# Expert blocks in a new order, and expert weights in half-size pieces

## Chip, cores and metric

The kernel runs on one core of a Trainium2 chip. The metric is the device time of one execution in microseconds (us). Engines are called as in the profile: PE multiplies (PEld loads its weights), DVE and ACT are the two engines for elementwise work on SBUF and PSUM, POOL is a slower third one that also issues indirect transfers, SP issues the plain transfers. Sixteen DMA engines move the data.

## The reference, cut to what matters

The reference is two transformer blocks on 1024 tokens of width 1024. Everything up to the last step (projections, convolution, a recurrent branch, attention, the router) is untouched here. The last step is a mixture of 32 experts. Each token goes to its two best experts; tokens are grouped by expert into blocks of 128 rows, and a block is computed as

```
def expert_block(args):
    xb, e = args
    hb = jax.nn.silu(xb @ w_gate[e]) * (xb @ w_up[e])     # 128x1024 @ 1024x256, twice
    return hb @ w_down[e]                                  # 128x256 @ 256x1024
```

after which each token's two results are weighted and added to the residual.

## The kernel before, in words

The expert step is phase_m. It always runs 33 blocks: one for each expert e = 0 to 31 (the first 128 tokens routed to it), and one, number 32 = NE, for the first expert that got more than 128. A loop under a run-time condition does further blocks; with these inputs it isn't entered.

A block needs 3 MB of float32 weights, 1 MB for each of gate, up and down, of which every partition gets 8 KB in one run. Products are made at near float32 accuracy from float32r halves: every operand x is split into h, a rounded copy (ACT, L1502 and L99), and l = x - h (DVE, L1503 and L100), and the product is h·h + h·l + l·h. The steps of a block, with the names of the profile:

- gather: POOL fetches the block's 128 token rows by index into mx (L1591, three buffers).
- moe_in: PE transposes mx in eight pieces (L1517); ACT and DVE split the result into xh and xl.
- weight_split: for gate, up and down in turn, SP issues the load of 1 MB into a buffer mw (L1608, three buffers in all), ACT makes gh or dh, DVE makes the rest ml (five buffers). For block 0 POOL does the subtraction in DVE's place; for block 32 the loads are indirect transfers issued by POOL (L1599).
- moe_up: 8 steps of four products each into one PSUM bank (L1529, L1531 twice, L1532); then ACT's silu (L1534) and DVE's product (L1535) give hb.
- moe_down: two transposes of hb (L1544), a split into hh and hl, twelve products into two PSUM banks (L128 to L130), each evicted to my by ACT (L1553); POOL scatters the rows to Y (L1595).

The program order is: prepare block e+1 (moe_in, the gather for e+2, all three weights), moe_up of e+1, moe_down of e. The framework that builds the program takes this order as a priority and reorders each engine's instructions by when it reckons them ready, so an engine's queue isn't exactly the program order; but once built, each engine and each issuing queue works strictly in its own order, and an instruction that waits holds up those behind it. A load can be issued only when the mw buffer that it takes has been read by both ACT and DVE. PSUM gives three banks named pm, which moe_up and moe_down share.

Before phase_m stands the router, a long chain of small DVE operations that ends in the token lists; the loads and splits of block 0 run beside it. route_rest, which places the tokens beyond the first 128 of an expert, is issued with block 6. After the last block, combine loads Y (8 MB), adds and stores the result (L1565 to L1570).

Of the kernel before, what the change touches and what calls it, by code (L numbers as in the profile page):

```python
# [1401 lines left out]
def route_rest(g, r, rt):  # L1402
# [41 lines left out]
    v.tensor_copy(rt["wi"], oex)  # L1444
# [46 lines left out]
def weight_split(g, wp, raw, wraw, eng=None):  # L1491

    nc = g.nc
    gh = wp.tile([128, 8, 512], F32R, name="gh", tag="gh", bufs=2)
    dh = wp.tile([128, 2, D], F32R, name="dh", tag="dh", bufs=2)
    ls = []
    for i, (w, h) in enumerate((("gate", gh[..., :256]), ("up", gh[..., 256:]), ("down", dh))):
        rw = raw.tile([128, 2048], F32, name="mw", tag="mw", bufs=3)
        wraw(w, rw)
        split = lambda x: x.rearrange("p (a b) -> p a b", a=8 if i < 2 else 2)  # L1500
        l = split(raw.tile([128, 2048], F32R, name="ml", tag="ml", bufs=5))
        nc.scalar.activation(h, split(rw), AF.Copy)  # L1502
        (eng or nc.vector).tensor_tensor(l, split(rw), b32(h), op=OP.subtract)  # L1503
        ls.append(l)
    return gh, ls[:2], dh, ls[2]
# [17 lines left out]
def moe_up(g, mp, xs, ws):  # L1523
    nc = g.nc
    xh, xl = xs
    gh, gl = ws[:2]
    p = pm(g)
    for j in range(8):
        nc.tensor.matmul(p, xh[:, j], gh[:, j], start=j == 0, stop=False)  # L1529
        for i in range(2):  # L1530
            nc.tensor.matmul(p[:, i * 256:i * 256 + 256], xh[:, j], gl[i][:, j], start=False, stop=False)  # L1531
        nc.tensor.matmul(p, xl[:, j], gh[:, j], start=False, stop=j == 7)  # L1532
    hb = mp.tile([128, 256], F32, name="hb", tag="hb", bufs=3)
# [5 lines left out]
def moe_down(g, mp, hb, ws, ydst):  # L1539
    nc = g.nc  # L1540
    dh, dl = ws[2:]
    pt = pg(g, 2, 128)
    for j in range(2):
        nc.tensor.transpose(pt[:, j], hb.rearrange("p (f j) -> p j f", j=2)[:, j, :], g.ident)  # L1544
    hh = mp.tile([128, 2, 128], F32R, name="hh", tag="hh", bufs=2)
    hl = mp.tile([128, 2, 128], F32R, name="hl", tag="hl", bufs=2)
    split_psum(g, hh, hl, pt)
    y = mp.tile([128, D], F32, name="my", tag="my", bufs=2)
    for n in range(2):
        p = pm(g)  # L1550
        for j in range(2):
            mm3(nc, p, hh[:, j], hl[:, j], dh[:, j, HALF[n]], dl[:, j, HALF[n]], j == 0, j == 1)
        nc.scalar.activation(y[:, HALF[n]], p, AF.Copy)  # L1553
# [3 lines left out]
def combine(g, raw, rt, res, k0, dst):  # L1557
# [4 lines left out]
    for t in range(NT):  # L1562
        tag, bufs = ("mw", 3) if t < 3 else ("ml", 5)
        ys.append(raw.tile([128, 2, D], F32, name="fy", tag=tag, bufs=bufs))
        nc.sync.dma_start(ys[t], src[tcol(t)])  # L1565
    for t in range(NT):
        h = res(t)
        for k in range(2):
            nc.vector.scalar_tensor_tensor(h, ys[t][:, k], rt["c"][:, k0 + k, t:t + 1], h, op0=OP.mult, op1=OP.add)  # L1569
# [12 lines left out]
def phase_m(g, acc, r, rt, out, mp, wp, raw):  # L1582
# [4 lines left out]
          "down": ins["w_down"].rearrange("e (p j) f -> (e p) (j f)", j=2)}  # L1587

# [9 lines left out]
    def gathered(idx):  # L1598
        return lambda w, rw: nc.gpsimd.indirect_dma_start(out=rw, out_offset=None, in_=wv[w], in_offset=off(idx))  # L1599
# [3 lines left out]
    mx = [mp.tile([128, D], F32, name=f"mx{i}") for i in range(3)]  # L1603
# [3 lines left out]
    def prep(e):  # L1607
        src = gathered(rt["wi"][:, 0:1]) if e == NE else lambda w, rw: nc.sync.dma_start(rw, wv[w][tcol(e), :])  # L1608
        xs = moe_in(g, mx[e % 3], xt.pop() if xt else moe_xt(mp))
        if e < NE:  # L1610
            gather(mx[(e + 1) % 3], rt["tok"][:, e + 1:e + 2])
        return weight_split(g, wp, raw, src, nc.gpsimd if e < 1 else None), xs

    gather(mx[0], rt["tok"][:, 0:1])
    ws, xs = prep(0)
    hb = moe_up(g, mp, xs, ws)
    for e in range(NE + 1):
        if e == 6:
            route_rest(g, r, rt)
        cur = hb, ws  # L1620
        if e < NE:
            ws, xs = prep(e + 1)
# [240 lines left out]
```

## Time and profile before

| | us |
|---|---|
| median of 3 runs (2861.75 to 2862.96) | 2862.53 |
| the profiled execution, its own time | 2861.98 |
| its span, first to last instruction | 2860.3 |
| hb of block 0 made | 2446.6 |
| hb of block 32 made | 2816.1 |

The span is what the trace shows, the time is what is measured around it; they differ by 1.7 us. The distance of the two hb marks holds 32 blocks in steady work, 11.55 us each; before it lie the earlier phases and the start of the expert step, behind it the last moe_down and combine.

### The profile page before, as it was taken

Reading aid. Unit: us, or ns where it says so; the run is one execution under the profiler, and the core shown is the slowest. Engines: PE = TensorE matmul, PEld = TensorE weight load, DVE = VectorE, ACT = ScalarE, POOL = GpSimd, SP = SyncE. Lnnn points to the kernel's source line nnn. Section 1 sums busy time; section 2 is a strip of 40 time slices with the busy share of each in tenths; the row PEclk is TensorE's granted clock in tenths of the full one; section 3 lists DMA queues with packets and bytes.
Section 4 is the critical chain, followed back from the end, with each engine's and each line's share of the span. In section 5 each row is a group of like instructions: output and inputs, shape, how many; then the busy total and the mean of one; then the engine's idle time right before and its main releaser. Section 6 shows DMA issues by size and latency. Waiting matters only on the chain. (4 is left out here: it accounts for less than half of the span.)

```text
span 2860.3 us, 33815 instructions
## 1 busy us (share of the span) xinstructions
PE 2672.9 (93%) x13274; PEld 2213.2 (77%) x13274; DVE 1850.0 (65%) x2551; ACT 1151.8 (40%) x1703; POOL 272.1 (10%) x290
## 2 busy tenths in 40 slices
PE   8999999999899999999999999998899996889894
PEld 6888888888778888777888878997777774777773
DVE  5778988898873332366254241677777777777775
ACT  4112121112122221455244332556767653667672
POOL 3000000000000000020000000000111113312111
PEclk9999999999999999999999999999999998999997
DMA  3111111111135432431122241444122214788987
GB/s 136 44 37 38 54 50 39 43 52 45 37 110 188 174 118 67 155 118 63 65 65 70 81 166 47 154 136 164 62 86 78 71 36 170 262 284 301 318 318 273
DMA packets 107905, 341.34 MB, mean 119 GB/s; under 512 B 15072, under 2 KB 35808, under 8 KB 95072
## 3 DMA queue, kind: packets, MB, share of 16 engines
q1 hardware_dynamic: 97808, 319.22, 32.3%
q0 software_dynamic: 9936, 19.94, 2.0%
q8 instruction: 105, 1.72, 0.3%
q14 instruction: 56, 0.46, 0.1%
HBM read 272.52 MB, written 84.41 MB: 125 GB/s over the span
## 5 line engine op out<-in xcount | busy, mean ns | idle before, releaser
L122 ACT ACTIVATE wh<-wr 128x1024 fp32r<-128x1024 f32 (+2 forms) x161 | 164.5, 1023 | 560.8 <-PE pm L129 423.2
L123 DVE TENSOR_TENSOR wl<-wr,wh 128x1024 fp32r<-128x1024 f32 (+2 forms) x159 | 187.6, 1182 | 289.1 <-ACT wh L122 288.5
L128 PE MATMUL pm<-uh,wh 128*128 128x512 f32 x896 | 360.3, 402 | 5.1 <-DVE gz L449 4.2
L129 PE MATMUL pm<-ul,wh 128*128 128x512 f32 x896 | 356.7, 398 | 0.3 <-DVE ul L103 0.3
L130 PE MATMUL pm<-uh,wl 128*128 128x512 f32 x896 | 355.4, 397 | 0.0
L277 DVE SCALAR_TENSOR_TENSOR acc<-v,vec,acc 128x1024 f32<-128x1024 f32 x240 | 307.4, 1281 | 3.9
L128 PE MATMUL pm<-nth,wh 128*128 128x512 f32 (+1 forms) x656 | 261.2, 398 | 0.7 <-ACT nth L102 0.7
L130 PE MATMUL pm<-nth,wl 128*128 128x512 f32 (+1 forms) x656 | 260.5, 397 | 0.0
L129 PE MATMUL pm<-ntl,wh 128*128 128x512 f32 (+1 forms) x656 | 258.5, 394 | 0.0
L128 PEld LDWEIGHTS pm<-uh,wh 128*128 128x128 f32 x896 | 170.5, 190 | 41.0 <-DVE gz L449 4.6
L130 PEld LDWEIGHTS pm<-uh,wl 128*128 128x128 f32 x896 | 170.5, 190 | 35.4 <-issue 1.0
L129 PEld LDWEIGHTS pm<-ul,wh 128*128 128x128 f32 x896 | 170.6, 190 | 35.0 <-issue 1.4
L1503 DVE TENSOR_TENSOR ml<-mw,gh 128x2048 fp32r<-128x2048 f32 x64 | 146.4, 2290 | 44.3 <-ACT gh L1502 44.2
L1502 ACT ACTIVATE gh<-mw 128x2048 fp32r<-128x2048 f32 x66 | 126.4, 1917 | 65.0 <-DMA mw<-in_w_up 34.6
L129 PEld LDWEIGHTS pm<-ntl,wh 128*128 128x128 f32 (+1 forms) x656 | 122.1, 186 | 31.2
L130 PEld LDWEIGHTS pm<-nth,wl 128*128 128x128 f32 (+1 forms) x656 | 122.0, 186 | 30.9
L128 PEld LDWEIGHTS pm<-nth,wh 128*128 128x128 f32 (+1 forms) x656 | 122.1, 186 | 30.2 <-ACT nth L102 0.9
L100 DVE TENSOR_TENSOR ptl<-pa,pth 128x512 fp32r<-128x512 f32 (+4 forms) x160 | 100.4, 633 | 60.2 <-ACT pth L99 59.6
L1531 PEld LDWEIGHTS pm<-ml,xh 128*128 128x128 f32 x528 | 105.3, 200 | 38.3 <-DVE ml L1503 15.0
L1529 PE MATMUL pm<-gh,xh 128*128 128x512 f32 x264 | 111.6, 423 | 19.5 <-ACT my L1553 18.5
L1531 PE MATMUL pm<-ml,xh 128*128 128x256 f32 x528 | 117.8, 297 | 10.8 <-DVE ml L1503 10.8
L1532 PE MATMUL pm<-gh,xl 128*128 128x512 f32 x264 | 109.0, 413 | 0.0
(520 smaller groups left out, 5958.2 us busy)
## 6 DMA issues: line engine op xcount, KB each, us to landing
wr<-in_w_in SPq DMA_DIRECT2D x97, 512.0 KB
mw<-in_w_gate SPq DMA_DIRECT2D x32, 1024.0 KB
mw<-in_w_up SPq DMA_DIRECT2D x32, 1024.0 KB
mw<-in_w_down SPq DMA_DIRECT2D x32, 1024.0 KB
Y<-zero SPq DMA_DIRECT2D x4, 2048.0 KB
fy<-Y SPq DMA_DIRECT2D x8, 1024.0 KB
kd<-kv SPq DMA_DIRECT2D x32, 192.0 KB
qd<-qs SPq DMA_DIRECT2D x32, 192.0 KB
```

The lines of the kernel that those rows point to most:

```text
L100: nc.vector.tensor_tensor(l, src, b32(h), op=OP.subtract)
L122: nc.scalar.activation(h, raw, AF.Copy)
L123: (eng or nc.vector).tensor_tensor(l, raw, b32(h), op=OP.subtract)
L128: nc.tensor.matmul(out, lh, rh, start=first, stop=False)
L129: nc.tensor.matmul(out, lh, rl, start=False, stop=False)
L130: nc.tensor.matmul(out, ll, rh, start=False, stop=last)
L277: nc.vector.scalar_tensor_tensor(acc, v[:, j:j + T], w[:, j:j + 1], acc, op0=OP.mult, op1=OP.add)
L1502: nc.scalar.activation(h, split(rw), AF.Copy)
L1503: (eng or nc.vector).tensor_tensor(l, split(rw), b32(h), op=OP.subtract)
L1529: nc.tensor.matmul(p, xh[:, j], gh[:, j], start=j == 0, stop=False)
L1531: nc.tensor.matmul(p[:, i * 256:i * 256 + 256], xh[:, j], gl[i][:, j], start=False, stop=False)
L1532: nc.tensor.matmul(p, xl[:, j], gh[:, j], start=False, stop=j == 7)
```

## The change

The loop now looks two blocks ahead. In iteration e it brings and splits gate and up of block e+2, does the first half of moe_up of e+1, then the transposes and the split of hb of block e (moe_hidden, in the middle of moe_up), the second half of moe_up, then moe_in of e+2, then brings and splits down of e+1, then the products of moe_down of e. Each weight comes in two transfers of 512 KB, 4 KB a partition, into mw buffers of half the size (eight instead of three large ones), with eight ml buffers and one more of half the size instead of five large ones. The splits are done by halves too, so there are twice as many instructions on ACT and DVE for them, each on 1024 instead of 2048 elements a partition. mx has two buffers, not three. For block 32 the row index of the indirect loads is kept for either half (rt["wi"]). combine loads Y in 16 pieces of 512 KB instead of 8 of 1 MB.

```diff
--- before.py
+++ after.py
@@ -1441,7 +1441,10 @@
     v.tensor_reduce(oex, ib, axis=AX.X, op=OP.add)
     v.tensor_scalar(oex, oex, 31.0, None, op0=OP.min)
     v.scalar_tensor_tensor(oex, oex, 128.0, r["part"].to_broadcast([128, 16]), op0=OP.mult, op1=OP.add)
-    v.tensor_copy(rt["wi"], oex)
+
+    for half in range(2):
+        v.tensor_scalar(ib[:, 0, :16], oex, 2.0, float(half), op0=OP.mult, op1=OP.add)
+        v.tensor_copy(rt["wi"][:, half], ib[:, 0, :16])
     ibk = til("ibk", 8, 16)
     nc.gpsimd.iota(ibk, pattern=[[0, 8], [1, 16]], base=0, channel_multiplier=0, allow_small_or_imprecise_dtypes=True)
     pt = pm(g)
@@ -1488,21 +1491,29 @@
     slot_tokens(g, r, pt, rt, 32, 16)
 
 
-def weight_split(g, wp, raw, wraw, eng=None):
-
-    nc = g.nc
+def gate_up(g, wp, raw, wraw, eng=None):
+
     gh = wp.tile([128, 8, 512], F32R, name="gh", tag="gh", bufs=2)
+    return gh, [halved(g, raw, wraw, w, gh[..., i * 256:i * 256 + 256], 4, eng) for i, w in enumerate(("gate", "up"))]
+
+
+def down(g, wp, raw, wraw, eng=None):
     dh = wp.tile([128, 2, D], F32R, name="dh", tag="dh", bufs=2)
+    return dh, halved(g, raw, wraw, "down", dh, 1, eng)
+
+
+def halved(g, raw, wraw, w, h, n, eng):
     ls = []
-    for i, (w, h) in enumerate((("gate", gh[..., :256]), ("up", gh[..., 256:]), ("down", dh))):
-        rw = raw.tile([128, 2048], F32, name="mw", tag="mw", bufs=3)
-        wraw(w, rw)
-        split = lambda x: x.rearrange("p (a b) -> p a b", a=8 if i < 2 else 2)
-        l = split(raw.tile([128, 2048], F32R, name="ml", tag="ml", bufs=5))
-        nc.scalar.activation(h, split(rw), AF.Copy)
-        (eng or nc.vector).tensor_tensor(l, split(rw), b32(h), op=OP.subtract)
+    for half in range(2):
+        rw = raw.tile([128, 1024], F32, name="mw", tag="mw", bufs=8)
+        wraw(w, half, rw)
+        split = lambda x: x.rearrange("p (a b) -> p a b", a=n)
+        l = split(raw.tile([128, 1024], F32R, name="ml", tag="ml", bufs=9))
+        hh = h[:, half * n:half * n + n]
+        g.nc.scalar.activation(hh, split(rw), AF.Copy)
+        (eng or g.nc.vector).tensor_tensor(l, split(rw), b32(hh), op=OP.subtract)
         ls.append(l)
-    return gh, ls[:2], dh, ls[2]
+    return ls
 
 
 def moe_xt(mp):
@@ -1520,36 +1531,43 @@
     return xh, xl
 
 
-def moe_up(g, mp, xs, ws):
+def moe_up(g, mp, xs, ws, mid=None):
     nc = g.nc
     xh, xl = xs
-    gh, gl = ws[:2]
+    gh, gl = ws
     p = pm(g)
     for j in range(8):
         nc.tensor.matmul(p, xh[:, j], gh[:, j], start=j == 0, stop=False)
         for i in range(2):
-            nc.tensor.matmul(p[:, i * 256:i * 256 + 256], xh[:, j], gl[i][:, j], start=False, stop=False)
+            nc.tensor.matmul(p[:, i * 256:i * 256 + 256], xh[:, j], gl[i][j // 4][:, j % 4], start=False, stop=False)
         nc.tensor.matmul(p, xl[:, j], gh[:, j], start=False, stop=j == 7)
+        if j == 3 and mid:
+            mid()
     hb = mp.tile([128, 256], F32, name="hb", tag="hb", bufs=3)
     nc.scalar.activation(hb, p[:, :256], AF.Silu)
     nc.vector.tensor_tensor(hb, p[:, 256:], hb, op=OP.mult)
     return hb
 
 
-def moe_down(g, mp, hb, ws, ydst):
-    nc = g.nc
-    dh, dl = ws[2:]
+def moe_hidden(g, mp, hb):
+
     pt = pg(g, 2, 128)
     for j in range(2):
-        nc.tensor.transpose(pt[:, j], hb.rearrange("p (f j) -> p j f", j=2)[:, j, :], g.ident)
-    hh = mp.tile([128, 2, 128], F32R, name="hh", tag="hh", bufs=2)
-    hl = mp.tile([128, 2, 128], F32R, name="hl", tag="hl", bufs=2)
-    split_psum(g, hh, hl, pt)
+        g.nc.tensor.transpose(pt[:, j], hb.rearrange("p (f j) -> p j f", j=2)[:, j, :], g.ident)
+    hs = [mp.tile([128, 2, 128], F32R, name="h" + x, tag="h" + x, bufs=2) for x in "hl"]
+    split_psum(g, *hs, pt)
+    return hs
+
+
+def moe_down(g, mp, hs, ws, ydst):
+    nc = g.nc
+    hh, hl = hs
+    dh, dl = ws
     y = mp.tile([128, D], F32, name="my", tag="my", bufs=2)
     for n in range(2):
         p = pm(g)
         for j in range(2):
-            mm3(nc, p, hh[:, j], hl[:, j], dh[:, j, HALF[n]], dl[:, j, HALF[n]], j == 0, j == 1)
+            mm3(nc, p, hh[:, j], hl[:, j], dh[:, j, HALF[n]], dl[j][:, 0, HALF[n]], j == 0, j == 1)
         nc.scalar.activation(y[:, HALF[n]], p, AF.Copy)
     ydst(y)
 
@@ -1560,13 +1578,14 @@
     src = g.Y.rearrange("(k t) d -> t k d", k=2)
     ys = []
     for t in range(NT):
-        tag, bufs = ("mw", 3) if t < 3 else ("ml", 5)
-        ys.append(raw.tile([128, 2, D], F32, name="fy", tag=tag, bufs=bufs))
-        nc.sync.dma_start(ys[t], src[tcol(t)])
+        tag, bufs = ("mw", 8) if t < 4 else ("ml", 9)
+        ys.append([raw.tile([128, D], F32, name="fy", tag=tag, bufs=bufs) for _ in range(2)])
+        for k in range(2):
+            nc.sync.dma_start(ys[t][k], src[tcol(t), k])
     for t in range(NT):
         h = res(t)
         for k in range(2):
-            nc.vector.scalar_tensor_tensor(h, ys[t][:, k], rt["c"][:, k0 + k, t:t + 1], h, op0=OP.mult, op1=OP.add)
+            nc.vector.scalar_tensor_tensor(h, ys[t][k], rt["c"][:, k0 + k, t:t + 1], h, op0=OP.mult, op1=OP.add)
         nc.sync.dma_start(dst[tcol(t), :], h)
 
 
@@ -1585,6 +1604,9 @@
     wv = {"gate": ins["w_gate"].rearrange("e (p j) f -> (e p) (j f)", j=8),
           "up": ins["w_up"].rearrange("e (p j) f -> (e p) (j f)", j=8),
           "down": ins["w_down"].rearrange("e (p j) f -> (e p) (j f)", j=2)}
+    wh = {"gate": ins["w_gate"].rearrange("e (p h j) f -> (e p h) (j f)", h=2, j=4),
+          "up": ins["w_up"].rearrange("e (p h j) f -> (e p h) (j f)", h=2, j=4),
+          "down": ins["w_down"].rearrange("e (p h) f -> (e p h) f", h=2)}
 
     def gather(x, idx):
 
@@ -1596,47 +1618,70 @@
                                      oob_is_err=False)
 
     def gathered(idx):
-        return lambda w, rw: nc.gpsimd.indirect_dma_start(out=rw, out_offset=None, in_=wv[w], in_offset=off(idx))
+        return lambda w, half, rw: nc.gpsimd.indirect_dma_start(out=rw, out_offset=None, in_=wh[w], in_offset=off(idx(half)))
 
 
     xt = [moe_xt(mp)]
-    mx = [mp.tile([128, D], F32, name=f"mx{i}") for i in range(3)]
+    mx = [mp.tile([128, D], F32, name=f"mx{i}") for i in range(2)]
     for x in mx:
         nc.gpsimd.memset(x, 0.0)
 
-    def prep(e):
-        src = gathered(rt["wi"][:, 0:1]) if e == NE else lambda w, rw: nc.sync.dma_start(rw, wv[w][tcol(e), :])
-        xs = moe_in(g, mx[e % 3], xt.pop() if xt else moe_xt(mp))
-        if e < NE:
-            gather(mx[(e + 1) % 3], rt["tok"][:, e + 1:e + 2])
-        return weight_split(g, wp, raw, src, nc.gpsimd if e < 1 else None), xs
-
-    gather(mx[0], rt["tok"][:, 0:1])
-    ws, xs = prep(0)
-    hb = moe_up(g, mp, xs, ws)
+    def src(e):
+        if e == NE:
+            return gathered(lambda half: rt["wi"][:, half, 0:1])
+        return lambda w, half, rw: nc.sync.dma_start(rw, wv[w][tcol(e), half * 1024:half * 1024 + 1024])
+
+    def bring(e):
+        if e <= NE:
+            gather(mx[e % 2], rt["tok"][:, e:e + 1])
+
+
+    def ready(e):
+        x = moe_in(g, mx[e % 2], xt.pop() if xt else moe_xt(mp))
+        bring(e + 2)
+        return x
+
+    eng = lambda e: nc.gpsimd if e < 1 else None
+    for e in range(2):
+        bring(e)
+    gu = {0: gate_up(g, wp, raw, src(0), eng(0))}
+    dn = {0: down(g, wp, raw, src(0), eng(0))}
+    xs = {0: ready(0)}
+    gu[1] = gate_up(g, wp, raw, src(1))
+    hb = moe_up(g, mp, xs.pop(0), gu.pop(0))
+    xs[1] = ready(1)
     for e in range(NE + 1):
         if e == 6:
             route_rest(g, r, rt)
-        cur = hb, ws
+        hs = []
+        if e + 2 <= NE:
+            gu[e + 2] = gate_up(g, wp, raw, src(e + 2))
         if e < NE:
-            ws, xs = prep(e + 1)
-            hb = moe_up(g, mp, xs, ws)
-        moe_down(g, mp, *cur, lambda y: scatter(y, rt["row"][:, e:e + 1]))
+            hb = moe_up(g, mp, xs.pop(e + 1), gu.pop(e + 1), lambda hb=hb: hs.append(moe_hidden(g, mp, hb)))
+        else:
+            hs.append(moe_hidden(g, mp, hb))
+        if e + 2 <= NE:
+            xs[e + 2] = ready(e + 2)
+        if e < NE:
+            dn[e + 1] = down(g, wp, raw, src(e + 1))
+        moe_down(g, mp, hs[0], dn.pop(e), lambda y: scatter(y, rt["row"][:, e:e + 1]))
     combine(g, raw, rt, lambda t: acc[:, t], 0, out)
 
 
     n = nc.values_load(rt["more"][0:1, 0:1], min_val=0, max_val=15)
     with tc.If(n > 0):
-        cur, tmp = (r["pool"].tile([128, 3, 16], I32, name=n, tag=tag) for n, tag in (("cur", "ib"), ("curt", "sel")))
-        for i, x in enumerate((rt["tok"][:, 32:48], rt["wi"], rt["row"][:, 32:48])):
+        cur, tmp = (r["pool"].tile([128, 4, 16], I32, name=n, tag=tag) for n, tag in (("cur", "ib"), ("curt", "sel")))
+        for i, x in enumerate((rt["tok"][:, 32:48], rt["wi"][:, 0], rt["row"][:, 32:48], rt["wi"][:, 1])):
             nc.vector.tensor_copy(cur[:, i], x)
         with tc.For_i(0, n, 1):
             nc.vector.tensor_copy(tmp, cur)
             nc.vector.tensor_copy(cur[:, :, 0:15], tmp[:, :, 1:16])
-            ws = weight_split(g, wp, raw, gathered(cur[:, 1, 0:1]))
+            from_ = gathered(lambda half: cur[:, 2 * half + 1, 0:1])
+            gu = gate_up(g, wp, raw, from_)
+            dn = down(g, wp, raw, from_)
             gather(mx[0], cur[:, 0, 0:1])
-            hb = moe_up(g, mp, moe_in(g, mx[0], moe_xt(mp)), ws)
-            moe_down(g, mp, hb, ws, lambda y: scatter(y, cur[:, 2, 0:1]))
+            hb = moe_up(g, mp, moe_in(g, mx[0], moe_xt(mp)), gu)
+            moe_down(g, mp, moe_hidden(g, mp, hb), dn, lambda y: scatter(y, cur[:, 2, 0:1]))
         combine(g, raw, rt, lambda t: acc[:, t], 2, out)
 
 
@@ -1696,7 +1741,7 @@
                 nc.vector.tensor_scalar(t[:96], t[:96], -96 ** -0.5, None, op0=OP.mult)
             small[nm + "g"] = t
         rt = {"c": c.tile([128, 4, 8], F32, name="rtc"), "row": c.tile([128, NB], I32, name="rtr"),
-              "tok": c.tile([128, NB], I32, name="rtt"), "wi": c.tile([128, 16], I32, name="rtw"),
+              "tok": c.tile([128, NB], I32, name="rtt"), "wi": c.tile([128, 2, 16], I32, name="rtw"),
               "more": c.tile([1, 1], I32, name="rtm")}
         chs = ExitStack()
         with ExitStack() as s:
```

## Rows read from the trace of the kernel before

**Rows 1.** The page, 40 equal slices of the span: busy tenths of PE and of DMA.

```profile
PE   8999999999899999999999999998899996889894
DMA  3111111111135432431122241444122214788987
```

**Rows 2.** DVE's product hb: duration min/median/max in ns, first and last start in us.

```profile
L1535 DVE TENSOR_TENSOR hb<-pm,hb x33: 414/418/425, 2446.6 to 2816.1; 128x256 f32<-128x256 f32 x33
```

**Rows 3.** Busy time of stretches; last columns: granted PE clock, DMA share, GB/s.

```profile
2446.60:2816.10 369.50, 329.75 (x1720) 274.59 (x1719) 274.02 (x230) 253.50 (x250) 76.69 (x62) 0.95 0.85 300
...
2738.00:2753.00 15.00, 13.21 (x69) 10.79 (x69) 11.39 (x9) 11.58 (x13) 3.05 (x3) 1.00 0.97 373
...
2826.00:2856.00 30.00, 0.00 (x0) 0.00 (x0) 20.23 (x16) 0.00 (x0) 0.00 (x0) 0.50 1.02 408
...
4.00:12.00 8.00, 2.07 (x6) 0.87 (x6) 2.90 (x4) 5.66 (x9) 4.15 (x8) 1.00 1.02 411
```

**Rows 4.** Waits, 2446.6 to 2816.1: engine, line, releaser, total us, times, longest.

```profile
DVE ml L1503 <- ACT gh L1502: 44.2, 39, 4.1
...
ACT gh L1502 <- DMA mw<-in_w_up: 31.6, 17, 4.4
ACT gh L1502 <- DMA mw<-in_w_gate: 23.2, 20, 2.2
PEld pm L1529 <- ACT my L1553: 23.1, 11, 3.9
```

**Rows 5.** Timeline, SP, ACT and DVE: one mw buffer's round.

```profile
2642.82 0.33 SPq L1608 DMA_DIRECT2D mw<-in_w_gate  x1
...
2651.13 1.92 ACT L1502 ACTIVATE gh<-mw 128x2048 fp32r<-128x2048 f32 x1 [1.59 <-DMA mw<-in_w_gate]
...
2653.09 2.29 DVE L1503 TENSOR_TENSOR ml<-mw,gh 128x2048 fp32r<-128x2048 f32 x1 [1.16 <-ACT gh L1502]
...
2655.41 0.33 SPq L1608 DMA_DIRECT2D mw<-in_w_gate  x1
```

**Rows 6.** Timeline and stretches around one PE stall.

```profile
2606.34 1.91 ACT L1502 ACTIVATE gh<-mw 128x2048 fp32r<-128x2048 f32 x1 [2.29 <-DMA mw<-in_w_up]
2608.16 0.37 ACT L1534 ACTIVATE hb<-pm 128x256 f32<-128x256 f32 x1
2608.42 0.59 ACT L1553 ACTIVATE my<-pm 128x512 f32<-128x512 f32 x1
...
2609.06 0.50 PE L1529 MATMUL pm<-gh,xh 128*128 128x512 f32 x1 [1.90 <-ACT my L1553]
...
2610.00:2617.00 7.00, 6.37 (x20) 5.46 (x21) 6.34 (x5) 4.23 (x3) 1.01 (x1) 0.52 0.81 274
```

**Rows 7.** Groups by form: busy us, mean ns, idle before; large splits, then half-size ones.

```profile
L1503 DVE TENSOR_TENSOR ml<-mw,gh 128x2048 fp32r<-128x2048 f32 x62 | 141.8, 2290 | 44.3 <-ACT gh L1502 44.2
L1502 ACT ACTIVATE gh<-mw 128x2048 fp32r<-128x2048 f32 x62 | 118.8, 1917 | 56.4 <-DMA mw<-in_w_up 31.6 <-DMA mw<-in_w_gate 23.2 <-DMA mw<-in_w_up,rtw 1.4
...
L123 DVE TENSOR_TENSOR wl<-wr,wh 128x1024 fp32r<-128x1024 f32 x118 | 144.0, 1222 | 199.1 <-ACT wh L122 198.8
...
L122 ACT ACTIVATE wh<-wr 128x1024 fp32r<-128x1024 f32 x117 | 124.0, 1060 | 404.3 <-PE pm L129 287.1 <-PE pm L130 79.2 <-issue 14.2
...
L1599 POOL DMA_INDIRECT mw<-in_w_up,rtw x1 | 1.0, 983 | 0.3 <-issue 0.3
```

**Rows 8.** Start of the expert step: router operations (min/median/max ns), POOL's splits, first moe_up.

```profile
L1330 DVE TENSOR_SCALAR eq<-oe,part x2: 349/2473/4597, 2400.7 to 2420.7; 128x256 bf16<-128x256 f32 x2
...
L1332 DVE TENSOR_SCALAR eq<-oe x4: 221/226/4525, 2398.8 to 2421.0; 128x128 bf16<-128x128 f32 x4
...
L1337 DVE TENSOR_TENSOR ek<-row,rkk x2: 1226/2931/4636, 2410.6 to 2422.2; 128x1024 bf16<-128x1024 f32 x2
...
2400.41 9.28 POOL L1503 TENSOR_TENSOR ml<-mw,gh 128x2048 fp32r<-128x2048 f32 x2 [4.78 <-ACT gh L1502]
...
2437.60 0.79 PE L1529 MATMUL pm<-gh,xh 128*128 128x512 f32 x1
```

## Prediction

> **What bounds the kernel now.** First the page's slices [rows 1]. PE is busy nine tenths nearly everywhere, with DMA mostly at one to four tenths; only in the last six slices does DMA rise to seven to nine tenths, while PE shows eight and nine until combine in the last. So the expert step is the one place where the two compete, and the change touches nothing else. Then the marks of hb [rows 2]: 369.5 us for 32 blocks, 11.55 us a block. Then the busy time of that stretch, the first row of [rows 3], which I read as four floors, each the time a block would take if that resource never waited:
>
> - DMA: share 0.85, so 0.85 x 11.55 = 9.82 us. At 300 GB/s a block moves 3.46 MB, 3.15 of it weights.
> - PE: busy 329.75 us, but at a mean granted clock of 0.95; the 5% are stretches at the lower level (1.2 GHz instead of 2.4), which cost 0.05 x 369.5 = 18.5 us. At full clock: (329.75 - 18.5) / 32 = 9.73 us.
> - DVE: 274.02 / 32 = 8.56 us. ACT: 253.50 / 32 = 7.92 us.
>
> No resource is full, and the block takes 1.7 us more than the highest floor. The waits [rows 4] say why: ACT stands 54.8 us for weights that haven't landed (31.6 and 23.2), DVE stands behind ACT, and PE stands 23.1 us for ACT's eviction my. The round of one mw buffer [rows 5] shows the loop behind it: the load goes out at 2642.82, the split can start at 2651.13, 8.31 us later, DVE is done with the buffer at 2655.38, and only then, at 2655.41, does the next load go out. Three buffers in such a round mean that for over 4 of 12.6 us each of them has no load in flight. How that reaches PE is in [rows 6]: ACT waits 2.29 us for the up weights, silu and my stand behind that split in ACT's queue, PE gets its PSUM bank only at 2609.06 after 1.90 us of idling, and then runs seven microseconds at a granted clock of 0.52, the lower level. A late load costs PE twice.
>
> **The change part by part.**
>
> *More, smaller buffers.* Eight halves are 4.19 MB of landing room instead of 3.15, and a half is held for 1.06 + 1.22 us of splitting [rows 7] instead of 1.92 + 2.29. Six halves make a block, so a buffer's round may last 8/6 of a block, 14 us at 10.5 us a block; with today's 8.31 us from issue to split it needs 8.31 + 2.28 = 10.6 us. Loads are then issued 3.4 us ahead of need, and DMA can approach a full share.
>
> *Order.* Gate and up of block e+2 are split during moe_up of e+1, a block earlier than now; the transposes for x and for hb are made where PE has other products on both sides. So the evictions that stand behind a late split have most of a block to spare, and [rows 6] should become rare. The same products and transposes run, so PE's floor stays 9.73 us.
>
> *Price of the halves.* DVE pays 3 x (2 x 1.222 - 2.290) = 0.46 us a block, ACT 3 x (2 x 1.060 - 1.917) = 0.61 us [rows 7]: floors of 9.02 and 8.53 us, still below DMA. SP issues three more loads a block at 0.33 us [rows 5], 1 us on a queue that otherwise waits for buffers. Were they not hidden, that would be 32 us in all.
>
> *Rows of 4 KB instead of 8 KB.* The trace before has no such weight load. Bounds: the expert stretch now moves 300 / 0.85 = 353 GB/s per full share; where transfers of 512 KB and 4 KB a partition fill the engines, they run at 411 GB/s (4 to 12 us), and combine at 408 [rows 3]. Those rows mix no gathers in, so I take no gain from them and no loss: 9.82 us stays the DMA floor.
>
> On this the Trainium skill (DMA: Bandwidth & Descriptors, Rules for kernel authors and Anatomy of one DMA) speaks against the change: it asks for at least 1 MiB a transfer and fits, for transfers that POOL issues, about 2.0 us plus bytes / 436 GB/s to each. By that two halves would cost 6.4 us where a whole one costs 4.4, an estimate of 6 us more a block if transfers ran one at a time, and a total near 3050 us. The full share at 411 GB/s with 512 KB transfers doesn't show this price where several are in flight.
>
> *How near the floor.* Nothing in the trace says what share a well fed DMA reaches here; it lies between 0.85 (no better than now) and the 1.02 of the two filled stretches. The 15 us from 2738 show 0.97 with three buffers when nothing got stuck [rows 3]. I take the middle of the ends, 0.935: 9.82 / 0.935 = 10.50 us a block, 1.05 us less, **33.6 us** over 32 blocks. PE would be 93% busy, which the earlier slices show to be common. Ends: 0, and (11.55 - 9.73) x 32 = 58 us, where PE's floor stops it.
>
> *Start.* POOL's subtraction for block 0 blocks some router operations on DVE: L1330, L1332 and L1337 took 4.60, 4.53 and 4.64 us once, and 0.35, 0.22 and 1.23 us when POOL was idle [rows 8], 12.0 us lost in a chain at whose end stands the first moe_up at 2437.60. POOL's pieces are now half as long (9.28 / 4 = 2.3 us), so an operation caught behind one waits half as long: at most 6.0 us back. But block 1's splits, now in four pieces, can slip into the same chain; I take half, **3.0 us**, ends 0 and 6.
>
> *The rest at nothing.* The three additional index operations of route_rest and its one mx buffer less are under 1 us, beside loads. For block 32 POOL issues six indirect loads for three, 3 x 0.98 us more [rows 7], hidden since POOL is busy 77 of 369 us [rows 3]; uncovered, 3 us. combine's loads move the same bytes at a share of 1.02, so eight issues more change nothing.
>
> Sum, on the profiled execution's own time: 2861.98 - 33.6 - 3.0 = 2825.4; the median of the runs is 0.55 higher: **2826 us**.
>
> **Rivals.**
>
> *DMA or PE is truly filled.* Both reach their floors, 9.8 to 10.2 us a block. For it: four floors that differ by little and a lookahead of two blocks. Against: with everything near full, any hiccup hits somebody. 1.55 us x 32 = 50, with the start 3: about 2809 us. Chance 0.15.
>
> *Only part of it.* PE's stalls halve but keep occurring, and each still brings the lower clock: 11.1 us a block, 14 us less, with the start 2845 us. Chance 0.12.
>
> *It doesn't do what it says.* The weights are late because the engines are slowed by gathers and scatters among them, not because loads are issued late; then a load issued earlier only stands longer in line, the share stays 0.85 and so does the block: 2859 to 2863 us. Against: 373 GB/s at 0.97 in the stretch from 2738. Chance 0.06.
>
> *Slower: the ninth ml buffer.* Gate and up of two blocks and down of one are ten halves, and there are nine. So the fourth subtraction of block e+2 must wait until the first half of moe_up of e+1 has freed one, and in DVE's queue hl, hb and xl can stand behind it, all of which PE needs. moe_up is 24 of a block's 36 full-width products, so a half of it is at most a third of PE's 9.73 us, 3.2 us. If DVE stands still that long each block, the block takes 9.02 + 3.2 = 12.2 us: 0.7 x 32 = 22 us slower, near 2884 us. It decides from 11.55 - 9.02 = 2.53 us of standing a block. Against: DVE already idles (369.5 - 274.0) / 32 = 2.98 us a block, the wait ends in mid moe_up, while hl is wanted only after its end, and PE's half doesn't depend on what waits. Chance 0.11. That 512 KB transfers pay a price of their own, so that a half stays over 13.1 us between issue and split (from there eight buffers hold a block above 11.55 us), I give 0.01.
>
> **How the numbers follow.** 0.55 for the forecast (10.2 to 10.8 us a block, 2816 to 2836 us), the rest as above. The measurement can tell about 0.2%, 6 us, from no change. Faster: 0.55 + 0.15 + 0.12 = 0.82; within: 0.06; slower: 0.12. The range runs from 2800 (58 + 6 less gives 2798) to 2858, and leaves out the last two kinds, 0.18.
>
> **What would show it.** Right: hb marks 336 us apart; DMA share near 0.93 and a granted clock of 0.98 or more between them; ACT's waits on mw cut by half or more; L1330, L1332 and L1337 at most 2.5 us and the first moe_up near 2435; SP's loads issued well before their split. Wrong: the splits of DVE waiting on PE (the ninth buffer), an unchanged share with longer landing times, or PE waiting for hl or xl in place of my.

## The result, and the profile after

| | before | after |
|---|---|---|
| device time, median (us) | 2862.14 (4 runs, 2855.66 to 2862.96) | 2810.26 (4 runs, 2808.89 to 2811.3) |
| ratio, 95% interval | 1 | 0.9828 [0.9814, 0.9842] |
| profiled execution, span (us) | 2861.98, 2860.3 | 2810.12, 2808.4 |
| hb(0) to hb(32), us a block | 369.5, 11.55 | 320.7, 10.02 |

The kernel got 1.7% faster: 52 us, where 36 were forecast. On the profiled executions the account is: the expert step's first hb comes 3.8 us earlier (2446.6 to 2442.8), the 32 blocks after it take 48.8 us less, and what follows the last hb takes 44.9 us for 44.2; 3.8 + 48.8 - 0.7 = 51.9, and 2861.98 - 2810.12 = 51.9.

The 3.8 us can't be put down to the change. The router's first operation L1297 stands at the start of the expert step, behind code that the change doesn't touch. Its line in the kernel before, in the changed kernel, and in the changed kernel run once more (after_again, below):

```profile
L1297 DVE TENSOR_TENSOR lg<-pm,rbias x2: 294/296/298, 2393.3 to 2415.2; 128x144 f32<-128x144 f32 x2
L1297 DVE TENSOR_TENSOR lg<-pm,rbias x2: 297/302/307, 2387.5 to 2399.6; 128x144 f32<-128x144 f32 x2
L1297 DVE TENSOR_TENSOR lg<-pm,rbias x2: 298/303/308, 2390.9 to 2403.2; 128x144 f32<-128x144 f32 x2
```

In the profiled execution the code ahead of it was 5.8 us faster, and between the two executions of the changed kernel it differs by 3.4. From L1297 to hb(0) it took 53.3 us before and takes 55.3 and 55.0 now: the start lost 2 us, and the gain lies in the blocks alone.

The page of the changed kernel, 40 equal slices, busy tenths of PE and DMA, as in [rows 1]:

```profile
PE   8999999999899999999999999999899999599993
DMA  3111111111025524422122124255222212699996
```

Where DMA used to go up and down between seven and nine tenths, it now stays at nine until the last slice, most of which is combine. The slice in which PE shows only five is the step's start, and DMA shows six there because loading begins.

The marks of hb, as in [rows 2], and four of the 33 in the timeline (start, duration, engine, line):

```profile
L1548 DVE TENSOR_TENSOR hb<-pm,hb x33: 404/418/426, 2442.8 to 2763.5; 128x256 f32<-128x256 f32 x33
2458.49 0.42 DVE L1548 TENSOR_TENSOR hb<-pm,hb 128x256 f32<-128x256 f32 x1
2729.58 0.42 DVE L1548 TENSOR_TENSOR hb<-pm,hb 128x256 f32<-128x256 f32 x1
2738.63 0.42 DVE L1548 TENSOR_TENSOR hb<-pm,hb 128x256 f32<-128x256 f32 x1
2754.93 0.42 DVE L1548 TENSOR_TENSOR hb<-pm,hb 128x256 f32<-128x256 f32 x1
```

The four are blocks 2, 29, 30 and 31. From 2 to 29 a block takes 271.09 / 27 = 10.04 us, most of them 9.3 to 10.7. Block 31 takes 16.3.

Busy time of stretches, columns as in [rows 3]; the first row is hb(0) to hb(32), the second the steady part of it, the third one a stall near the end:

```profile
2442.80:2763.50 320.70, 310.49 (x1724) 266.18 (x1724) 284.92 (x337) 266.76 (x345) 92.75 (x66) 0.99 0.92 344
2460.00:2735.00 275.00, 269.39 (x1505) 230.54 (x1505) 251.75 (x299) 234.83 (x304) 81.23 (x57) 1.00 0.97 365
2743.50:2750.30 6.80, 5.21 (x18) 4.71 (x19) 4.79 (x4) 6.80 (x10) 2.46 (x2) 0.50 0.63 258
```

In the steady part DMA's share is 0.97 and PE's granted clock 1.00, where the mean before was 0.95 [rows 3]. Share times block is 0.97 x 10.04 = 9.74 us, so the block now stands almost on what DMA takes for it. The prediction's 9.82 us can't be set beside this figure: it is the mean from hb(0) to hb(32), at 300 GB/s x 11.55 us = 3.46 MB a block, while the steady part moves 365 x 10.04 = 3.66 MB a block. The stretch's first 17 us stand at a share of 0.75 and its last 28.5 us, with few loads left, at 0.54. Over the same stretch as before, DMA's time a block is now 0.92 x 10.02 = 9.22 us, at the same 3.45 MB: a full share is worth 344 / 0.92 = 374 GB/s, where it was worth 353.

Waits of 2442.8 to 2763.5, as in [rows 4]:

```profile
ACT dh L1513 <- DMA mw<-in_w_down: 21.1, 34, 1.3
...
PEld pm L1543 <- DVE xl L100: 7.5, 14, 1.0
...
ACT gh L1513 <- DMA mw<-in_w_gate,rtw: 5.4, 1, 5.4
...
ACT gh L1513 <- DMA mw<-in_w_gate: 4.9, 12, 0.8
...
ACT gh L1513 <- DMA mw<-in_w_up: 2.2, 8, 0.6
...
DVE ml L1514 <- PE pm L1542: 1.8, 1, 1.8
```

ACT's 54.8 us for gate and up became 7.1 (4.9 + 2.2). It still waits 21.1 us for down (6.8 before), in 34 pieces of at most 1.3 us, and once 5.4 us for block 32; for all three weights and block 32 these are 33.6 us, where it was 63.0. But nothing that PE needs stands behind them for long: PE's 23.1 us for my are gone, and its largest wait in total is 7.5 us, for xl. The last row is the ninth ml buffer: once, 1.8 us.

The round of a load, beside [rows 5]: gate's two halves go out at 2646.42, and the split of the first is

```profile
2646.42 2.02 SPq L1632 DMA_DIRECT2D mw<-in_w_gate  x2
...
2657.64 1.06 ACT L1513 ACTIVATE gh<-mw 128x1024 fp32r<-128x1024 f32 x1 [0.21 <-DMA mw<-in_w_gate]
```

11.2 us after the issue (the split of another gate half, at 2647.85, is too near to be this load's), where a whole one took 8.31. The load goes out far ahead and is still only just in time: it stands in line behind other loads. That is what a stretch looks like in which the transfers set the pace.

ACT's queue in the steady part, beside [rows 6]:

```profile
2605.43 0.37 ACT L99 ACTIVATE hh<-pg 128x256 fp32r<-128x256 f32 x1
2606.29 1.06 ACT L1513 ACTIVATE dh<-mw 128x1024 fp32r<-128x1024 f32 x1 [0.49 <-DMA mw<-in_w_down]
2607.26 0.36 ACT L1547 ACTIVATE hb<-pm 128x256 f32<-128x256 f32 x1
2607.62 1.06 ACT L1513 ACTIVATE gh<-mw 128x1024 fp32r<-128x1024 f32 x1
2608.59 1.01 ACT L99 ACTIVATE xh<-pa 128x1024 fp32r<-128x1024 f32 x1
2609.50 1.05 ACT L1513 ACTIVATE gh<-mw 128x1024 fp32r<-128x1024 f32 x1
2610.45 0.58 ACT L1571 ACTIVATE my<-pm 128x512 f32<-128x512 f32 x1
2610.92 1.06 ACT L1513 ACTIVATE gh<-mw 128x1024 fp32r<-128x1024 f32 x1
2611.87 0.59 ACT L1571 ACTIVATE my<-pm 128x512 f32<-128x512 f32 x1
```

Between any two of these operations that serve PE (hh, silu, xh, my, my) stands one split of 1.06 us; before, two of 1.92 us could stand there, as between hh at 2600.51 and silu at 2608.16. None of those shown here waits for PE.

### The profile page after: what moved, and what is told of

The parts are those of the page before. It is cut to its first block, busy times and chain, and to the rows that moved or that the text cites. A ratio compares the mean times of both kernels' runs of the same rounds, so it can differ in the third digit from the quotient of the medians.

```text
span 2808.4 us, 34388 instructions
## 1 busy us (share of the span) xinstructions
PE 2648.5 (94%) x13274; PEld 2199.4 (78%) x13274; DVE 1861.2 (66%) x2650; ACT 1160.7 (41%) x1802; POOL 286.1 (10%) x295
## 5 line engine op out<-in xcount | busy, mean ns | idle before, releaser
L130 PEld LDWEIGHTS pm<-uh,wl 128*128 128x128 f32 x896 | 169.7, 189 | 35.2 <-issue 1.0
L1514 DVE TENSOR_TENSOR ml<-mw,gh 128x1024 fp32r<-128x1024 f32 x128 | 152.6, 1220 | 14.9 <-ACT gh L1513 10.9
L1513 ACT ACTIVATE gh<-mw 128x1024 fp32r<-128x1024 f32 x132 | 138.5, 1063 | 22.6 <-DVE rkk L1336 7.7
L1543 PE MATMUL pm<-gh,xl 128*128 128x512 f32 x264 | 108.4, 411 | 16.5 <-DVE xl L100 16.3
L1542 PE MATMUL pm<-ml,xh 128*128 128x256 f32 x528 | 107.1, 284 | 0.0
```

What stands on the lines that cost most here:

```text
L130: nc.tensor.matmul(out, ll, rh, start=False, stop=last)
L1513: g.nc.scalar.activation(hh, split(rw), AF.Copy)
L1514: (eng or g.nc.vector).tensor_tensor(l, split(rw), b32(hh), op=OP.subtract)
```

## The experiments

At first three explanations of the gain stood against each other: room (4 MB of landing room for 3), order (two blocks ahead), and the size of the pieces. A fourth question was what sets the new pace, DMA or PE. Times are compared as ratios to the kernel before on the same chip; us a block and share (DMA, GB/s) are from hb(0) to hb(32), each from one profiled execution.

| kernel | what it is | median us | ratio, 95% | us a block | share, GB/s |
|---|---|---|---|---|---|
| before | | 2862.14 | 1 | 11.55 | 0.85, 300 |
| halves_old_order | pieces and room, not the order | 2861.17 | 1.0023 [1.001, 1.0036] | 11.60 | 0.85, 298 |
| order_whole_mw3 | the order alone | 2855.42 | 0.9995 [0.9984, 1.0007] | 11.39 | 0.87, 308 |
| whole_load_half_split | order, splits by halves | 2840.9 | 0.9948 [0.9928, 0.9968] | 10.98 | 0.89, 319 |
| half_loads_whole_buf | and loads by halves | 2826.57 | 0.9891 [0.9873, 0.9908] | 10.41 | 0.93, 336 |
| halves_mw6 | and buffers by halves, 3 MB | 2814.99 | 0.9854 [0.9832, 0.9876] | 10.04 | 0.94, 348 |
| after_again | the change, 4 MB | 2814.56 | 0.9841 [0.9825, 0.9858] | 10.06 | 0.92, 343 |
| halves_x_ahead | halves, only x ahead | 2849.59 | 0.9982 [0.9968, 0.9997] | 11.17 | 0.87, 309 |
| less_pe | after, less PE work | 2810.49 (one) | | 9.96 | 0.95, 350 |
| less_dma | after, less loading | 2801.14 (one) | | 9.39 | 0.77, 258 |
| dve0 | after, no splits on POOL | 2812.88 | 0.9842 [0.9822, 0.9863] | 10.14 | |
| dve0_tail | and block 29's scatter later | 2811.89 | 0.9834 [0.9812, 0.9856] | 10.23 | |
| rest_mid | after, block 32 in the middle | 2821.53 | 0.9872 [0.9854, 0.989] | 10.08 | |

### The pieces without the order: halves_old_order

```diff
+    def prep(e):
+        xs = moe_in(g, mx[e % 2], xt.pop() if xt else moe_xt(mp))
...
+        return gate_up(g, wp, raw, src(e), eng(e)), down(g, wp, raw, src(e), eng(e)), xs
...
+            gu, dn, xs = prep(e + 1)
+            hb = moe_up(g, mp, xs, gu)
+        moe_down(g, mp, moe_hidden(g, mp, cur[0]), cur[1], lambda y: scatter(y, rt["row"][:, e:e + 1]))
```

> The old order of the loop (prepare block e+1, moe_up of e+1, moe_down of e) with the new weights: halves of 512 KB, eight mw and nine ml half buffers, two mx. Theory R (the room and the quick release of the landing buffers keep DMA full, the order adds little): most of the 52 us, 2812 to 2825 us, DMA share between the first and last hb at 0.90 or more. Theory O (the lookahead takes PE and the evictions out of the way of late splits, and DMA fills up only because splits then come in time): less than half of it, 2840 to 2860 us, share below 0.88, with PE still waiting for my.

Measured: 11.60 us a block, the time of before to 0.2%. Eight half buffers and nine ml halves give nothing in the old order. The waits of 2445 to 2816.3 say where the gain went:

```profile
ACT hb L1547 <- PE pm L1543: 53.6, 26, 4.6
...
ACT gh L1513 <- DMA mw<-in_w_gate: 39.2, 16, 3.7
...
PEld pm L1540 <- ACT xh L99: 23.9, 15, 3.0
```

and its timeline shows one turn of it, first ACT, then PE:

```profile
2663.58 1.06 ACT L1513 ACTIVATE gh<-mw 128x1024 fp32r<-128x1024 f32 x1 [3.09 <-DMA mw<-in_w_gate]
...
2666.45 1.02 ACT L99 ACTIVATE xh<-pa 128x1024 fp32r<-128x1024 f32 x1
...
2675.77 0.38 ACT L1547 ACTIVATE hb<-pm 128x256 f32<-128x256 f32 x1 [3.31 <-PE pm L1543]
2676.05 2.00 ACT L1513 ACTIVATE gh<-mw 128x1024 fp32r<-128x1024 f32 x2
...
2667.53 0.50 PE L1540 MATMUL pm<-gh,xh 128*128 128x512 f32 x1 [2.48 <-ACT xh L99]
```

ACT stands 3.09 us for a load, with xh behind it; PE stands for xh and then runs its next products with starts 0.43 us apart where 0.23 is usual; ACT then reaches silu and stands 3.31 us for PE, with the splits of the next halves behind it (they run at once at 2676.05, so they had landed, and they hold their buffers meanwhile). Two engines wait in turn for each other through one queue. A full share here is worth 298 / 0.85 = 351 GB/s, before it was 353: rows of 4 KB cost nothing.

### The order without the pieces: order_whole_mw3

```diff
-    for half in range(2):
-        rw = raw.tile([128, 1024], F32, name="mw", tag="mw", bufs=8)
-        wraw(w, half, rw)
...
+    rw = raw.tile([128, 2048], F32, name="mw", tag="mw", bufs=MWB)
+    wraw(w, rw)
...
+    l = split(raw.tile([128, 2048], F32R, name="ml", tag="ml", bufs=5))
```

(MWB is 3.)

> The new order of the loop with the old weights: transfers of 1 MB, three mw and five ml buffers of full size. Theory R: the landing room is that of before, so nearly nothing is won, 2850 to 2865 us, share 0.83 to 0.87. Theory O: most of the 52 us, 2812 to 2830 us, share 0.90 or more.

Measured: 11.39 us a block, and the time of before within its interval. The waits of 2445.5 to 2810:

```profile
ACT dh L1511 <- DMA mw<-in_w_down: 27.7, 21, 3.1
ACT gh L1511 <- DMA mw<-in_w_up: 24.2, 19, 2.8
ACT gh L1511 <- DMA mw<-in_w_gate: 21.2, 17, 2.9
PEld pm L1537 <- ACT my L1568: 17.6, 10, 2.9
```

ACT stands 73 us for loads, more than before (54.8 and 6.8 for down), and PE still stands for my behind it. So neither part does anything by itself, and both together take 1.6 to 1.7% off.

### The steps between: whole_load_half_split, half_loads_whole_buf, halves_mw6

All three have the new order. The first keeps loads of 1 MB into three whole buffers and splits each in halves:

```diff
+    rw = raw.tile([128, 2048], F32, name="mw", tag="mw", bufs=MWB)
+    wraw(w, rw)
...
+        hh, x = h[:, half * n:half * n + n], split(rw[:, half * 1024:half * 1024 + 1024])
```

> The new order with loads of 1 MB into three whole mw buffers, as before, but with the splits by halves into nine half ml buffers. Theory S (the short splits are what the order needs: evictions stand behind 1 us instead of 2 us, and a block's parts interleave finely): 1.3 to 1.9% faster than the kernel before, about 10.1 us a block. Theory L (small landing buffers that come free one by one are what it needs; with three whole ones loads still go out late): 0 to 0.6% faster, above 11.0 us a block, ACT still waiting 50 us or more for loads.

The second loads by halves too, but a pair still shares one of three whole buffers, which comes free only when both are split:

```diff
+    rw = raw.tile([128, 2048], F32, name="mw", tag="mw", bufs=MWB)
+    for half in range(2):
+        wraw(w, half, rw[:, half * 1024:half * 1024 + 1024])
```

> The new order with loads of 512 KB and splits by halves, but every two halves land in one of three whole mw buffers, which comes free only when both halves have been split. If the size of the load is what mattered between whole loads (10.98 us a block) and halves with the same 3 MB of room (10.04 us): near 10.1 us a block, 1.3 to 1.7% faster than the kernel before. If the release of the buffer half by half is what mattered: 10.7 to 11.1 us a block, 0.4 to 0.8% faster.

The third has half buffers, but six, the 3 MB of before:

```diff
-        rw = raw.tile([128, 1024], F32, name="mw", tag="mw", bufs=8)
+        rw = raw.tile([128, 1024], F32, name="mw", tag="mw", bufs=6)
```

> The changed kernel with six half mw buffers in place of eight, the 3 MB of landing room of before. Theory R: a good part is lost again, 2825 to 2845 us, share 0.87 to 0.90, ACT waiting for loads 10 us or more longer. Theory O: 2808 to 2818 us, as with eight.

Measured, in order: 10.98, 10.41 and 10.04 us a block; the second lies between the two values that were expected, so the size of the load and the release by halves both count. ACT's and DVE's busy time is the same in all three (265, 268, 267 us; 284, 286, 284), and the share rises: 0.89, 0.93, 0.94. From 11.39, splitting by halves gives 0.41 us a block, loading by halves 0.57, giving buffers back by halves 0.37, and the fourth megabyte nothing (10.04 against 10.02 and 10.06). (The ratios of the last two steps touch, 0.9873 and 0.9876; beside half_loads_whole_buf on the same chip the change itself is 12.0 us faster, 2826.57 against 2814.56, which is 0.37 us a block.) Room is refuted: at equal room the pieces give it all. ACT's waits for loads fall along the same steps, from 76.6 us in the first (35.2 down, 23.8 up, 17.6 gate) to 53.0 in the second (18.2, 17.1, 17.7). Between order_whole_mw3 and the first they don't fall (73.1 to 76.6), so what the half splits give there isn't shown by these waits; which one it is stays open.

The Trainium skill (DMA: Bandwidth & Descriptors, Rules for kernel authors) asks for 1 MiB or more a transfer. The first two kernels differ in this: loads of 1 MB against 512 KB into the same buffers, so that a half can also be split as soon as it has landed. The small loads win by 0.57 us a block. The rule's price isn't seen, and the measurement decides.

### Which part of the order: halves_x_ahead

```diff
+    gu, dn = weights(0)
+    xs = ready(0)
+    hb = moe_up(g, mp, xs, gu)
+    xs = ready(1)
...
+            gu, dn = weights(e + 1)
+            hb = moe_up(g, mp, xs, gu)
```

Halves, with x made ready a block earlier, but weights and hb where they were.

> Halves, the old order for the weights (all of block e+1 before its moe_up) and for hb, but x two blocks ahead: gather, transposes and split of x for e+2 right after moe_up of e+1. If PE's stall on xh and xl was what held the old order with halves at the old time (45 us of its waits): 1.2 to 1.8% faster than the kernel before. If gate and up must be split a block earlier, so that ACT has splits to do that wait for nothing of PE: less than 0.8% faster.

Measured: 11.17 us a block, so x alone takes off 0.43 of the 1.58 us between halves_old_order and the change. The waits of 2442 to 2799.5:

```profile
ACT gh L1513 <- DMA mw<-in_w_gate: 71.6, 35, 4.4
...
PEld pm L128 <- ACT hh L99: 28.7, 26, 3.2
```

PE no longer waits for xh, but for hh, which in ACT's queue comes after the late gate split and the splits that it has pushed back. The rest needs gate and up a block earlier, the transposes of hb inside moe_up, or both; these two were not tried apart.

### What sets the pace: less_pe, less_dma

```diff
-        nc.tensor.matmul(p, xl[:, j], gh[:, j], start=False, stop=j == 7)
+        if j == 7:
+            nc.tensor.matmul(p, xl[:, j], gh[:, j], start=False, stop=True)
```

> The changed kernel without the product of xl and gh in moe_up for seven of the eight steps, so that PE has 7 x 0.23 = 1.6 us less to do a block, and with all loads. If DMA sets the pace of a block now (share 0.97 in the steady stretch): 9.8 to 10.0 us a block, 2803 to 2811 us. If PE sets it (no gap over 0.8 us there): 8.5 to 9.2 us a block, 2770 to 2785 us.

```diff
+    for half in range(2):
+        rw = raw.tile([128, 1024], F32, name="mw", tag="mw", bufs=8)
+        wraw("gate", half, rw)
+        for i in range(2):
...
+            g.nc.scalar.activation(hh, split(rw), AF.Copy)
```

> The changed kernel without the loads of up: the splits of up read the raw gate weights, so DMA has a third of the weight bytes less to move, and ACT, DVE and PE do the same work. If DMA sets the pace and PE stands close behind it: 9.75 to 9.9 us a block, PE without a gap, DMA share near 0.7. If DVE or ACT is what holds a block at 10.0 us: 10.0 us a block still, with PE waiting for splits.

Windows of hb(0) to hb(32), less_pe:

```profile
2445.00:2763.70 318.70, 275.77 (x1491) 230.90 (x1491) 283.08 (x341) 262.61 (x343) 94.36 (x66) 0.96 0.95 350
```

and less_dma:

```profile
2450.80:2751.20 300.40, 300.40 (x1716) 262.20 (x1715) 282.38 (x334) 255.56 (x342) 91.54 (x64) 1.00 0.77 258
```

Taking 35 us of work off PE changes the block by 0.06 us; taking a third of the weights off DMA brings it to 9.39 us, with PE busy without a gap. So DMA sets the pace of the changed kernel, and PE's own floor is 9.39 us, 0.6 below (and below the 9.75 to 9.9 us that were expected).

### The two ends: dve0, dve0_tail, rest_mid, after_again

```diff
-    eng = lambda e: nc.gpsimd if e < 1 else None
+    eng = lambda e: None
```

> The changed kernel with block 0's subtractions on DVE instead of POOL. In the changed kernel one router operation of DVE (L1456) took 12.5 us beside POOL's subtractions and the first full moe_up waited for DVE's xl. If that block is what sets the start: L1456 at 0.4 us, hb of block 0 made 4 to 8 us earlier, the whole 4 to 8 us (0.15 to 0.3%) faster than the changed kernel. If the loads set the pace from the start: the first hb earlier, the last hb where it was, 0 to 2 us.

Block 0's subtractions go to DVE. L1456, held for 12.49 us in the changed kernel (shown below), takes 0.41, and from the router's first L1297 (2391.1) to hb(0) (2440.2) it takes 49.1 us for 55.3. Yet the 32 blocks then take 324.4 us for 320.7, and the ratio is that of the change. Of the 6.2 us that the start gains, the blocks give back 3.7, and the times don't show the rest.

```diff
+            for y in late:
+                scatter(y, rt["row"][:, e - 1:e])
...
+        moe_down(g, mp, hs[0], dn.pop(e), late.append if e == NE - 3 else lambda y: scatter(y, rt["row"][:, e:e + 1]))
```

> As dve0, and the scatter of block 29 is issued behind the indirect weight loads of block 32 on POOL's queue instead of ahead of them, so that these loads don't wait for block 29's products. If the 4.6 us PE stall near the end of the changed kernel and its stretch at the lower clock come from these late loads: 4 to 9 us faster than dve0, no gap of PE over 2 us between the hb of blocks 29 and 32. If the loads are late for the buffers they land in: 0 to 2 us.

This was to let block 32's indirect loads go out ahead of block 29's scatter. In the built queue the scatter still came first (2736.52, the loads from 2738.19), and PE's gap at block 31 is still there, 4.7 us. It didn't test what it was meant to.

```diff
+    at = lambda p: p if p < MID else NE if p == MID else p - 1
...
-        moe_down(g, mp, hs[0], dn.pop(e), lambda y: scatter(y, rt["row"][:, e:e + 1]))
+        moe_down(g, mp, hs[0], dn.pop(e), lambda y: scatter(y, rt["row"][:, at(e):at(e) + 1]))
```

> The changed kernel with block 32, whose weights POOL loads by index, done as the 17th block instead of the last. In the changed kernel DMA falls to a share of 0.54 and PE stands 4.6 us near the end, when these late loads are the only ones left. If loads of other blocks that SP issues fill the gap in mid stream: 4 to 9 us faster than the changed kernel. If the late loads hold up everything behind them wherever they are: 0 to 2 us.

Block 32 as the seventeenth. The long block moves with it: between the marks of hb at 2578.41 and 2595.79 lie 17.4 us, where at the end it is 16.3. The indirect loads hold up what is behind them wherever they stand. The median is 7.0 us above that of the change itself on the same chip, though the intervals just touch, so nothing is gained and perhaps something lost. The changed kernel beside it, once more:

> The changed kernel once more, to be compared with the other kernels of this call: 1.6 to 1.8% faster than the kernel before.

10.06 us a block, ratio 0.9841 for 0.9828 the first time; by the medians the gain is 44.6 us here (2859.15 to 2814.56) and 51.9 there. No kernel tried here that does all the work beats the changed one by more than these two differ.

## Why the prediction was right or wrong

- *Direction and mechanism: right.* Loads go out earlier, ACT's waits for gate and up fall by far more than half (with down's and block 32's, from 63.0 to 33.6 us, by a little under half), PE's stalls behind my and with them the lower clock go away: a clock of 0.99 between the marks, as forecast, and a DMA share of 0.92 for 0.93. That PE waits for xl in place of my, named as a sign of being wrong, did come, but at 7.5 us for 23.1.
- *How near the floor: the term that was mis-sized is the floor, not the share.* The sum was 9.82 / 0.935 = 10.50 us a block, 33.6 us. Over the same stretch the share came out at 0.92, a little below 0.935, but DMA's time a block at 9.22 us: 9.22 / 0.92 = 10.02 us, 48.8 us. The bytes are the same, so "9.82 us stays the DMA floor" is the step that failed: 0.85 x 11.55 us took the 353 GB/s of a DMA that isn't full for what a full share can move, and it moved 374. The row for it was at hand: 373 / 0.97 = 385 GB/s in the 15 undisturbed microseconds from 2738 [rows 3]. That the middle of 0.85 and 1.02 came so near the measured share is luck, for it mixes 0.97 in the steady part with 0.75 and 0.54 at the two ends. The rival "DMA or PE is truly filled", 9.8 to 10.2 us and 2809 us at a chance of 0.15, is what came about, with DMA almost filled; PE's own floor isn't reached.
- *Buffers: right in effect, wrong in reason.* The step argued from eight buffers a round. Six do as well (halves_mw6). What counts is that a piece is loaded, split and given back in small steps, worth 11.39 - 10.04 = 1.35 us a block in the new order and nothing in the old one.
- *Order: right, but it was argued as an aid to the buffers.* It is a condition: without it the pieces are worth nothing.
- *PE's floor: 9.73 was too high.* 9.39 (less_dma): busy time less what the lower clock costs overstates the work by 0.3 us a block, and why isn't settled. It did no harm, since DMA's floor lies above.
- *Halves on ACT and DVE: right.* In the steady part the splits took 1.065 and 1.220 us (page: 1063 and 1220 ns as means), priced at 1.060 and 1.222.
- *4 KB rows at nothing: right for the rows by themselves.* In the old order a full share is worth 351 GB/s with them and 353 without. That it is worth 374 in the changed kernel comes with the order and the pieces together; by what, isn't shown.
- *Start: wrong, 2 us lost where 3.0 were to be gained; the earlier hb(0) is luck.* From L1297 to hb(0) it takes 55.3 us for 53.3. L1330, L1332 and L1337 weren't halved, but freed altogether: POOL's splits come later now. Another operation is caught instead (next fence), for 12.1 us where the three had lost 12.0, and PE's first moe_up stands 11.8 us for the xl behind it. The step that failed is that a caught operation waits for one of POOL's pieces at most. Where the other 2 us go wasn't traced.
- *Block 32's loads, put at nothing: wrong, and small.* The rows below. POOL issues the first at 2734.59, right behind a scatter; ACT gets the gate half 5.37 us late, xh stands behind it, PE stands 4.60 us and then runs 6.8 us at 0.50 (the third window row above), about 3.4 us more. Block 31 is 6.3 us over the mean of blocks 3 to 29. Before, PE's longest wait between hb(30) and hb(32) was 0.96 us. The last three blocks take 33.9 us, before 32.8: of the gain of the others they have none.
- *The ninth ml buffer, the rival on the other side: 1.8 us once.* The argument against it held: DVE has the time.

The start: groups of lines L1330, L1332, L1337 as in [rows 8], and the one that is caught now:

```profile
L1330 DVE TENSOR_SCALAR eq<-oe,part x2: 346/348/349, 2394.9 to 2405.2; 128x256 bf16<-128x256 f32 x2
...
L1332 DVE TENSOR_SCALAR eq<-oe x4: 217/224/226, 2393.0 to 2405.4; 128x128 bf16<-128x128 f32 x4
...
L1337 DVE TENSOR_TENSOR ek<-row,rkk x2: 1224/1225/1226, 2396.2 to 2406.7; 128x1024 bf16<-128x1024 f32 x2
...
L1456 DVE TENSOR_TENSOR sel<-oe,i x2: 412/6452/12493, 2415.3 to 2500.9; 128x256 f32<-128x256 f32 x2
```

The end, timeline of POOL, ACT and PE around block 31:

```profile
2732.92 1.36 POOL L1617 DMA_INDIRECT Y<-my,rtr  x1 [3.58 <-ACT my L1571]
2734.59 1.12 POOL L1621 DMA_INDIRECT mw<-in_w_gate,rtw  x1 [0.30 <-issue]
...
2743.07 1.06 ACT L1513 ACTIVATE gh<-mw 128x1024 fp32r<-128x1024 f32 x1 [5.37 <-DMA mw<-in_w_gate,rtw]
2744.04 1.00 ACT L99 ACTIVATE xh<-pa 128x1024 fp32r<-128x1024 f32 x1
...
2745.09 0.79 PE L1540 MATMUL pm<-gh,xh 128*128 128x512 f32 x1 [4.60 <-ACT xh L99]
```

What stays open: why a full share moves more when DMA is fed better; whether block 32's loads would be in time if they went out ahead of the scatter; how the order's worth divides between gate and up a block ahead and hb's transposes inside moe_up; and which wait the half splits shorten when loads and buffers stay whole.

## What to carry to other kernels

Where one queue holds both the work on landing data and the evictions that another engine waits for, looking further ahead and cutting the pieces smaller can each be worth nothing and together all there is: try them together before dropping either. Read a resource's floor in a stretch of the trace where that resource is full: share times time where it wasn't full came out 6.5% too high for DMA here (9.82 for 9.22 us), and busy time less the slow clock 3.6% too high for PE (9.73 for 9.39). Measure a gain from a mark inside the part that was changed, since the code ahead of it varied by 3.4 us between two executions of one kernel. And before adding buffers, cut the ones there are: three megabytes in six pieces did here what four did in eight.

## What the runs showed of the hardware

A DVE operation with two SBUF inputs that takes 0.41 us alone (dve0) took 12.49 us beside POOL's subtractions (12.51 in after_again). In the timeline POOL runs five of them in a row meanwhile:

```profile
2415.33 12.49 DVE L1456 TENSOR_TENSOR sel<-oe,i 128x256 f32<-128x256 f32 x1
2415.96 6.98 POOL L1514 TENSOR_TENSOR ml<-mw,gh 128x1024 fp32r<-128x1024 f32 x3
...
2422.91 4.62 POOL L1514 TENSOR_TENSOR ml<-mw,dh 128x1024 fp32r<-128x1024 f32 x2
```

DVE's ends at 2427.82, POOL's fifth at 2427.53. The prediction had priced a caught operation at one of POOL's pieces at most, 2.3 us; shorter pieces don't shorten such a wait when the next piece follows at once. The Trainium skill (SBUF — State Buffer, SBUF: two separate sides) describes a lock on a port that the two engines share, held by whichever starts first for its whole instruction; this trace agrees that one of them is shut out, but DVE was shut out for five instructions here, not for one, and its record starts 0.63 us before the first of them.

A full share of the DMA engines isn't worth the same in all kernels. From hb(0) to hb(32) it is 335 GB/s in less_dma (258 / 0.77), 351 to 355 in before, halves_old_order, order_whole_mw3 and halves_x_ahead (shares of 0.85 to 0.87), 358 and 361 in whole_load_half_split and half_loads_whole_buf, and 370 to 374 in halves_mw6 and the changed kernel (0.92 to 0.94). By and large it rises with the share; what makes it so no run here separates.
